# One transformer-style layer on one core: conditioning products on VectorE, complex products by three real ones, another order of steps

## The chip, the cores and the metric

The kernel runs on one core of a Trainium2 chip. The metric is the device time of one execution in microseconds (us). The engines are TensorE (matmul; PE in the rows, its weight loads PEld), VectorE (DVE), ScalarE (ACT), GpSimd (POOL) and SyncE (SP), which here only issues loads. Each engine runs its own queue in order and waits on semaphores for the others.

## The reference

One layer over 256 latent tokens and 256 context tokens of width 1024, all in fp32:

```
mod  = silu(c) @ w_mod + b_mod           # six vectors: shift1, scale1, gate1, shift2, scale2, gate2
h    = layer_norm(x) * (1 + scale1) + shift1          # the context likewise, with c_ctx
u, q, k, v, gates = split(h @ w_in)      # widths 512, 1024, 256, 256, 2048
y    = two-way S5 scan of u (32 groups, 64 complex states), started from the context's last states
ssm  = (gelu(y) @ w_glu_a) * sigmoid(gelu(y) @ w_glu_b)
att  = attention(q, k, v; latent and context keys) @ w_attn_o
x    = post_norm(alpha * x + gate1 * ((s1 * ssm + s2 * att) @ w_out))        # s1, s2 = sigmoid(gates)
m    = layer_norm(x) * (1 + scale2) + shift2
x    = post_norm(alpha * x + gate2 * moe(m))   # 32 experts, a token goes to 2 of them
```

The context needs shift1 and scale1 only; shift2, scale2, gate1 and gate2 are products of `c` alone ("c-only").

## The kernel before, in words

The program has two phases. The first, everything up to the routing, is written as some 45 generators ("streams"), such as `loads`, `mod2`, `w2_flow`, `scan`, `dense`, `outputs`, `prefetch4`. A stream yields `ask(engine, tiles, ...)` ahead of each step, and class `Flow` resumes one stream at a time. Which one is a fixed list of stream numbers, `ORDER`; where each tile lies in the area of SBUF is a second list, `PLACE` (NS places of 4 KB a partition). So the order of each engine's queue, and of the loads in SP's, is decided when the program is built. All engine calls of this phase pass through one helper, so their rows carry one line, L273.

The parts that matter here:

- `mod_loads` and `mod_cols` (L437 to L606) make the mod vectors. For each of 12 groups TensorE multiplies 16 blocks of w_mod (256 columns) by a 32-column tile that holds silu of c and of c_ctx (`scp`), in fp32, two passes each; ScalarE copies the result (`mr`), TensorE turns it by four transposes, VectorE sums the parts (`msum`) and adds the bias. `mod1` does the four groups of shift1 and scale1; `mod2` the eight c-only groups.
- `s5_powers`, `w1_flow`, `w2_flow` (L705 to L906) build the scan's matrices on VectorE: 16 blocks, each a complex product of powers (`pin`, `pout`) with b or c, as six operations of 128x512.
- The dense products (`dense`, L1238) run as three matmuls on fp32r halves. `split` makes the halves: ScalarE copies the high one, VectorE subtracts for the low one, TensorE then takes both.
- `u_turn` (L673) sends u through DRAM (`uscr`) with loads on POOL's queue. `outputs` (L993) turns each block of the scan's output on TensorE, writes it to DRAM (`yscr`) and reads it back as `yT`, where ScalarE applies GELU.
- `prefetch8`, `prefetch2`, `prefetch4` and `refill` load 18 pieces of expert weights, 1 MB each, into places as they come free.

The second phase (from L1861) is a loop over 16 pairs of experts. For each pair: the gate product (`into(p, 0)`, tiles `gu`), the combination of the last pair's result, the up product (`into(p, 1)`), the dispatch of the next pair's tokens, the down product (`down_of`, tiles `y`); `reload` issues the next weights as places come free. In the last pair `ln2_row` (L1852) spreads the final norm's gain and bias over the partitions by one-row matmuls, and `overflow` (L1756) holds a branch that handles experts with too many tokens. Then the final norm runs on VectorE and four stores end the program.

Of the kernel before, what the change touches and what calls it, by code (L numbers as in the profile page):

```python
# [86 lines left out]
class Flow:  # L87
# [247 lines left out]
def build(ctx, tc, I, out):  # L335
# [549 lines left out]
    def w1_flow():  # L885
        for b in range(8):
# [1125 lines left out]
```

## Time and profile before

| | us |
|---|---|
| time, median of 3 runs (lowest, highest) | 813.92 (812.88, 816.1) |
| the profiled execution, its own time | 813.46 |
| its span in the trace | 811.6 |
| busy: TensorE, VectorE, ScalarE, POOL | 762.1, 370.8, 294.2, 30.9 |

Mean granted TensorE clock 0.984 of full speed; HBM read 265.79 MB. Times in rows are us from the span's start unless marked ns. A busy share is an average over stages that are limited by different things, so the stages have to be read apart. An engine's idle time is shown with the instruction that ended it ("<-"); matmuls overlap, so their busy time can be a little over the time from start to start.

### The profile page before, as it was taken

How to read it: one execution, taken by the hardware profiler on the slowest of the kernel's cores; microseconds unless marked ns; L12 is line 12 of the kernel's file. 1: busy time of each engine (PE TensorE's matmuls, PEld its weight loads, DVE VectorE, ACT ScalarE, POOL GpSimd, SP SyncE). 2: the span in 40 equal slices, each digit the busy share in tenths (PEclk: the TensorE clock that was granted, in tenths of full speed). 3: DMA queues.
4: the chain of work that ended last, by engine and by line, in shares of the span. 5: the costliest groups of instructions: out<-in, count | busy, mean ns of one | idle time of the engine just before them, and what ended most of it. 6: DMA issues, size and time to landing. Idle time of an engine off the chain costs nothing. (4 is left out here: it accounts for less than half of the span.)

```text
span 811.6 us, 11217 instructions
## 1 busy us (share of the span) xinstructions
PE 762.1 (94%) x4371; PEld 435.6 (54%) x4371; DVE 370.8 (46%) x858; ACT 294.2 (36%) x573; POOL 30.9 (4%) x48
## 2 busy tenths in 40 slices
PE   3899989889999999899999999999999999999985
PEld 1678677657657787744444444444344434443422
DVE  6999978888634768723112211221222112211205
ACT  4552586856988543432212210221022102211210
POOL 0003312000000000200000000000000000000000
PEclk9999999999999999799999999999999999999998
DMA  9987364594478886959999999999999999999991
GB/s 352 350 303 262 87 231 137 212 333 136 152 181 333 329 286 240 367 187 391 423 422 422 421 420 421 420 419 422 422 420 420 422 421 420 422 420 420 422 372 53
DMA packets 52126, 269.70 MB, mean 332 GB/s; under 512 B 10082, under 2 KB 15586, under 8 KB 23268
## 3 DMA queue, kind: packets, MB, share of 16 engines
q1 hardware_dynamic: 46260, 265.28, 82.3%
q0 software_dynamic: 1152, 2.59, 1.1%
q10 hardware_dynamic: 4656, 1.05, 0.7%
q8 instruction: 37, 0.61, 0.3%
q14 instruction: 21, 0.17, 0.1%
HBM read 265.79 MB, written 3.11 MB: 331 GB/s over the span
## 5 line engine op out<-in xcount | busy, mean ns | idle before, releaser
L273 PE MATMUL gu<-b,b 128*64 128x512 f32 x1024 | 231.0, 597 | 3.4 <-DMA b<-in_w_exp_up_dram 2.6
L273 PE MATMUL acc<-b,b 128*128 128x512 f32 (+1 forms) x792 | 202.4, 390 | 4.4 <-DVE q L273 2.0
L273 PEld LDWEIGHTS acc<-b,b 128*128 128x128 f32 x792 | 136.5, 190 | 36.2 <-issue 9.2
L273 PEld LDWEIGHTS gu<-b,b 128*64 128x64 f32 x1024 | 73.3, 137 | 148.3 <-issue 138.6
L273 PE MATMUL y<-b,hT 128*64 128x512 f32 x512 | 113.4, 595 | 0.2 <-issue 0.2
L273 DVE TENSOR_TENSOR hh<-hh,gu 128x512 f32<-128x512 f32 (+1 forms) x17 | 11.0, 655 | 213.8 <-PE gu L273 193.0
L273 ACT ACTIVATE b<-y,modT 128x128 f32<-128x128 f32 x120 | 45.2, 456 | 138.5 <-PE y L273 138.5
L273 DVE TENSOR_TENSOR b<-b,b 128x1024 fp32r<-128x1024 f32 (+1 forms) x61 | 72.0, 1187 | 30.8 <-ACT b L273 29.7
L273 ACT ACTIVATE b<-b 128x1024 fp32r<-128x1024 f32 (+3 forms) x70 | 71.3, 1028 | 26.5 <-PE acc L273 24.2
L273 PEld LDWEIGHTS y<-b,hT 128*64 128x64 f32 x512 | 35.8, 137 | 66.5 <-issue 66.5
L273 PEld LDWEIGHTS y<-d,b 128*128 128x128 f32 x480 | 55.9, 192 | 12.2 <-issue 11.4
L273 PE MATMUL y<-d,b 128*128 128x128 f32 x480 | 60.0, 278 | 0.0
L273 ACT ACTIVATE yh<-b 128x512 fp32r<-128x512 f32 x31 | 19.5, 629 | 97.5 <-DVE b L273 97.5
L273 DVE SCALAR_TENSOR_TENSOR b<-y,wsl,b 128x512 f32<-128x512 f32 x32 | 24.0, 751 | 66.2 <-PE y L273 66.2
L273 ACT ACTIVATE hh<-gu 128x512 f32<-128x512 f32 x16 | 9.6, 597 | 117.0 <-PE gu L273 117.0
L273 ACT ACTIVATE b<-tr 128x512 f32<-128x512 f32 (+2 forms) x60 | 33.9, 583 | 49.4 <-PE tr L273 48.7
L273 PE MATMUL ss<-b,b 128*32 128x128 f32 (+2 forms) x344 | 36.9, 305 | 4.6 <-ACT b L273 2.9
L273 PE MATMUL acc<-b 128*128 128x512 f32 (+1 forms) x104 | 36.9, 368 | 0.0
L273 PEld LDWEIGHTS ss<-b,b 128*32 128x32 f32 (+1 forms) x344 | 25.9, 147 | 14.8 <-issue 8.7
L273 DVE TENSOR_TENSOR yl<-b,yh 128x512 fp32r<-128x512 f32 x31 | 21.5, 692 | 23.3 <-ACT yh L273 23.3
L273 PE MATMUL ss<-b,scp 128*32 128x256 f32 x384 | 26.8, 414 | 5.0 <-DMA b<-in_w_mod_dram 5.0
L273 PE MATMUL acc<-yh,cw 128*128 128x512 f32 x62 | 26.1, 421 | 0.0
(209 smaller groups left out, 675.7 us busy)
## 6 DMA issues: line engine op xcount, KB each, us to landing
b<-in_w_exp_gate_dram SPq DMA_DIRECT2D x64, 1024.0 KB, 19.8
b<-in_w_exp_up_dram SPq DMA_DIRECT2D x64, 1024.0 KB, 19.8
b<-in_w_exp_down_dram SPq DMA_DIRECT2D x63, 1024.0 KB, 19.8
b<-in_w_mod_dram SPq DMA_DIRECT2D x32, 512.0 KB, 7.0
b<-in_w_in_dram SPq DMA_DIRECT2D x14, 1024.0 KB, 7.7
b<-in_w_mod_dram SPq DMA_DIRECT2D x8, 1024.0 KB, 8.6
b<-in_w_attn_o_dram SPq DMA_DIRECT2D x4, 1024.0 KB, 5.3
b<-in_w_out_dram SPq DMA_DIRECT2D x4, 1024.0 KB, 5.0
```

What stands on the lines that cost most here:

```text
L273: return f(*args, **kw)
```

## The change

- **c-only products on VectorE.** `mod2` no longer uses TensorE. The c-only part of w_mod is stored transposed (`w_modT`, 32 tiles of 128x1024, 512 KB each); SP loads c once, spread over all partitions (`crow`), ScalarE applies SiLU, and 32 VectorE operations multiply a tile by it and sum along the row. The tiles are loaded from half of the scan on, into places of kind p4. `gate1`, `router_w` and `diag2` wait for the vectors that they use.
- **Complex products by three real ones.** Each of the 16 blocks takes one operation of 512 and two of 1024 elements a partition; sums and differences of the powers are made ahead (two operations on POOL, 12 copies on ScalarE, two on VectorE).
- **U by one load** of 1 MB on SP's queue in place of four on POOL's.
- **Gated output on TensorE.** The scan's output is gathered in `ya`, and eight transposes feed GELU straight from PSUM; `yscr` goes, and w_glu's rows are stored in the order that this gives.
- **Order and space.** New `ORDER` and `PLACE`, 46 places, still 18 prefetched pieces; the attention's output product may start once its first part is there.
- **The end.** The final norm's gain and bias come as two broadcast loads of 512 KB behind the last weights, not by `ln2_row`; the overflow test stands ahead of the last up product; in the final norm ScalarE sums one half of the tokens.

```diff
@@ mod_loads, mod2
-        for o in ((3, 4), (2, 5)):
-            for jp in range(4):
-                yield ask("Z", None, lambda: m_l[0] == 4, lambda: U, g4=4)
-                wm.append([[wload(w_mod, z * D + 256 * jp, 256, k0, 4, "g4") for k0 in (0, 4)] for z in o])
+        for z in (1, 2, 0, 3):
+            for j in range(KT):
+                yield ask("Z", None, lambda: m_l[0] == 4, lambda: g_n[0] >= 15, p4=1)
+                r = new("p4", [P, D], name="wr")
+                SY.dma_start(r, I["w_modT"][z * KT + j])
+                wm2.append(r)
...
-        for half in (1, 2):
-            for jp in range(4):
-                yield ask("T", None, lambda: mod_n[0] >= 4)
-                yield from mod_cols(half, jp)
+        yield ask("Y", None, lambda: m_l[0] == 4, lambda: g_n[0] >= 14, p4=1)
+        cb = new("p4", [P, D], name="cb")
+        bcast(cb, I["crow"], D)
+        yield ask("S", [cb], table=AF.Silu)
+        S.activation(cb, cb, AF.Silu)
+        for half, w in ((1, 0), (1, 1), (2, 0), (2, 1)):
+            sm = small.tile([P, KT], FT, name=f"msum{half}{w}", bufs=1)
+            for j in range(KT):
+                yield ask("V", lambda: [wm2[0], cb], lambda: wm2)
+                r = wm2.pop(0)
+                V.tensor_tensor_reduce(out=r, in0=r, in1=cb, scale=1.0, scalar=0.0, op0=OP.mult, op1=OP.add, accum_out=sm[:, j:j + 1])
+                free(r)
+            stt(modT[:, half, w, :, 0], sm, float(w if half < 2 else 0), bmodT[:, half, w], OP.add, OP.add)
+            md.add((half, w))
@@ w2_flow (w1_flow likewise)
-                for r in range(2):
-                    tt(t1, pr[0], cr[r], OP.mult)
-                    tt(w2[:, r], pr[1], cr[1 - r], OP.mult)
-                    if r == 0:
-                        tt(w2[:, 0], t1, w2[:, 0], OP.subtract)
-                    else:
-                        stt(w2[:, 1], t1, -1.0, w2[:, 1], OP.mult, OP.subtract)
+                tt(t1, pone[0][:, 0, i, :, :, None].to_broadcast(ps4), sums[0][:, 0, i, :, None, :].to_broadcast(ps4), OP.mult)
+                tt(w2.rearrange("p r g j c -> p (r g) j c"), pout[0][:, i].rearrange("p r g j -> p (r g) j")[:, :, :, None].to_broadcast(sh),
+                   s5c[0][:, i].rearrange("p r g c -> p (r g) c")[:, :, None, :].to_broadcast(sh), OP.mult)
+                tt(wf, wf, t1.rearrange("p g j c -> p (g j c)")[:, None, :].to_broadcast([P, 2, 512]), OP.add)
@@ u_turn
-        for i in range(4):
-            PL.dma_start(U[0][:, 8 * i:8 * i + 8], ...)
+        SY.dma_start(U[0], bass.AP(tensor=uscr.tensor, offset=uscr.offset, ap=[[64, P], [16 * 512, G], [1, 64]]))
@@ outputs
-                T.transpose(ps, yk, ident)
-                S.activation(ysb[:, 4 * b:4 * b + 4], ps.rearrange("p (g k) -> p g k", g=4), AF.Copy)
-            S.dma_start(bass.AP(tensor=yscr.tensor, ...), ysb)
-        S.dma_start(y_, yscr.rearrange("(i p) t -> p i t", p=P))
-        S.activation(y_, y_, AF.Gelu_apprx_tanh)
+                S.activation(ya[:, :, 4 * f + b], ps.rearrange("p (j c) -> p j c", j=8), AF.Copy)
+        for z in range(2):
+            for j in range(4):
+                T.transpose(ps[:, j], ya[:, 4 * z + j].rearrange("p g c -> p (g c)"), ident)
+            S.activation(yv[:, 4 * z:4 * z + 4], ps.rearrange("p j (i k) -> p j i k", i=4), AF.Gelu_apprx_tanh)
@@ the last pair and the end
+        else:
+            overflow(gu_p.tile([P, F], FT, name="gu"))
         into(p, 1, range(UB))
-        if not more:
-            for i in range(3):
-                lnp = ln2_row(i, gu_p if i == 2 else y_p)
         into(p, 1, range(UB, KT))
...
-            overflow(lnp)
+            ln2 = unit(D)[1]
+            for z in range(2):
+                bcast(ln2[:, z], I["ln2_b" if z else "ln2_g"], D)
...
+        S.activation(sq[n][:, 0:512], acc[1][n], AF.Copy, accum_out=s4[:, 0, n:n + 1])
+        S.activation(sq[n][:, 512:], acc[1][n], AF.Square, bias=mv[1][:, 1:2], accum_out=s4[:, 1, n:n + 1])
```

How the queues change, at three places. First TensorE, among the gate projections, where the scan's kernels (`kall`) are turned. Before (`scp` is the tile of silu of c, `mr` the copied result, `acc` the projections):

```order
L273 MATMUL acc<-b_117,b_247 128x512
L273 MATMUL ss<-b_107,bm 32x128 x8
L273 MATMUL ss<-b_107,scp 32x256 x4
L273 MATMUL ss<-b_113,scp 32x256 x4
L273 MATMUL ss<-b_123,scp 32x256 x4
L273 MATMUL ss<-b_337,scp 32x256 x4
L273 MATMUL tr<-kall,cst_78 128x64
L273 MATMUL acc<-b_117,b_336 128x512
L273 MATMUL acc<-b_458,b_336 128x512
L273 MATMUL acc<-b_117,b_247 128x512
L273 MATMUL tr<-cst,mr 128x128 x4
```

With the change, at the same turn of `kall`:

```order
L284 MATMUL acc<-b_290,b_513 128x512
L284 MATMUL acc<-b_348,b_513 128x512
L284 MATMUL tr<-kall,cst_78 128x64
L284 MATMUL acc<-b_210 128x512
L284 MATMUL acc<-b_211,b_210 128x512
L284 MATMUL acc<-b_210,b_211 128x512
```

The `scp` matmuls and `mr` transposes are gone from between the projections; the four groups of `mod1` are the only ones left, all in the first 113 entries of the queue.

Second VectorE with the change, in the attention stage behind the scan (`ISA` is the multiply-and-sum and, in the short rows, the reading of its sum into `msum`; `b_1561` is silu of c; the `TENSOR_TENSOR` rows of 128x1024 are low halves of splits):

```order
L284 TENSOR_TENSOR b_290<-b_1682,b_2272 128x1024
L284 ISA b_122,msum_2165<-b_122,b_1561 128x1024
L284 ISA msum_2165 128x1
L284 ISA b_425,msum_2165<-b_425,b_1561 128x1024
L284 RECIPROCAL sm<-sm 128x2
L284 TENSOR_TENSOR b_210<-b_425,b_2082 128x1024
L284 ISA b_105,msum_2165<-b_105,b_1561 128x1024
L284 SCALAR_TENSOR_TENSOR modT<-msum_2165,bmodT 128x8
L284 TENSOR_TENSOR b_2359<-b_1399,b_2359 128x1024
```

(Each multiply-and-sum is followed by such a short row; one stands here.) Before, no such rows stood between the low halves; 30 of the 32 stand behind the scan now.

Third SP, between the first expert loads. Before:

```order
L273 DMA b_115<-in_w_exp_gate_dram 128x2048
L273 DMA b_337<-in_w_glu_a_dram 128x2048
L273 DMA b_2709<-in_w_glu_b_dram 128x2048
L273 DMA count<-in_count_dram 128x256
L273 DMA rt<-in_wr_dram 128x288
L273 DMA rt<-in_br_dram 128x36
L273 DMA b_107<-in_w_exp_gate_dram 128x2048
L273 DMA b_1081<-in_w_exp_gate_dram 128x2048
L273 DMA b_575<-in_w_exp_up_dram 128x2048
```

With the change:

```order
L284 DMA b_2377<-in_w_modT_dram 128x1024
L284 DMA b_915<-in_w_exp_gate_dram 128x2048
L284 DMA b_441<-in_w_glu_b_dram 128x2048
L284 DMA b_207<-in_w_modT_dram 128x1024
L284 DMA b_1399<-in_w_glu_a_dram 128x2048
L284 DMA b_2448<-in_w_exp_gate_dram 128x2048
L284 DMA b_1637<-in_w_attn_o_dram 128x2048
L284 DMA b_425<-in_w_exp_up_dram 128x2048
L284 DMA b_151<-in_w_modT_dram 128x1024
```

The loads of `w_modT` stand between the expert loads and those of the glu weights; before, all of w_mod had been loaded ahead of them. Ten of the 18 expert loads come behind the last of them.

## Rows read from the trace of the kernel before

**Rows 1.** Windows by stage: us, busy of each engine (instructions), PEclk, DMA share, GB/s.
```profile
core 0: us, PE busy (x) PEld busy (x) DVE busy (x) ACT busy (x) POOL busy (x), PEclk, DMA share, GB/s
0.00:58.00 58.00, 39.68 (x373) 30.68 (x374) 49.29 (x147) 31.81 (x56) 2.52 (x8) 0.97 0.91 347
58.00:212.00 154.00, 144.20 (x1010) 108.42 (x1010) 133.51 (x359) 99.17 (x205) 22.29 (x32) 0.99 0.57 192
212.00:347.00 135.00, 127.67 (x706) 94.44 (x704) 83.40 (x153) 82.06 (x133) 4.99 (x6) 0.96 0.78 282
347.00:366.00 19.00, 17.96 (x94) 8.49 (x96) 4.00 (x16) 5.11 (x13) 0.00 (x0) 1.00 0.50 177
366.00:766.00 400.00, 398.54 (x2070) 181.21 (x2068) 86.57 (x161) 71.79 (x163) 0.00 (x0) 1.00 1.01 419
766.00:798.40 32.40, 30.17 (x119) 10.74 (x115) 4.39 (x8) 3.65 (x6) 0.00 (x0) 0.95 0.74 299
798.40:811.60 13.20, 3.90 (x11) 1.59 (x10) 9.68 (x17) 0.60 (x1) 1.10 (x2) 0.80 0.21 79
```
**Rows 2.** Windows again, the first microseconds of the first gate product.
```profile
350.00:354.00 4.00, 3.93 (x19) 1.40 (x20) 0.00 (x0) 1.06 (x4) 0.00 (x0) 1.00 0.01 4
```
**Rows 3.** Groups by line, TensorE, 58 to 213 us: xcount | busy, mean ns | idle before.
```profile
L273 PE MATMUL ss<-b,scp 128*32 128x256 f32 x256 | 16.1, 383 | 2.3 <-DMA b<-in_w_mod_dram 2.3
L273 PE MATMUL tr<-cst,mr 128*128 128x128 f32 x32 | 4.8, 274 | 0.0
```
**Rows 4.** Groups by line and form, VectorE and ScalarE (the second row: 212 to 347 us).
```profile
L273 DVE TENSOR_TENSOR wt<-pout,b 128x512 f32<-128x512 f32 x16 | 11.0, 687 | 0.2
L273 DVE TENSOR_TENSOR b<-b,b 128x1024 fp32r<-128x1024 f32 x30 | 36.5, 1224 | 27.9 <-ACT b L273 27.1 <-PE acc L273 0.5
L273 DVE SCALAR_TENSOR_TENSOR b<-b,dnv,b 128x1024 f32<-128x1024 f32 x2 | 2.6, 1276 | 0.0
L273 ACT ACTIVATION_READ_ACCUMULATOR pe<-acc,mx,rq 128x1 f32 x16 | 3.1, 196 | 0.0
L273 ACT ACTIVATE b<-ss 64x256 f32<-64x256 f32 x32 | 19.9, 622 | 6.0 <-PE ss L273 5.6
```
**Rows 5.** Timeline of VectorE, two places: start us, us, what, [idle before].
```profile
77.25 0.68 DVE L273 SCALAR_TENSOR_TENSOR b<-wt,b 128x512 f32<-128x512 f32 x1
77.85 0.68 DVE L273 TENSOR_TENSOR w<-wt,w 128x512 f32<-128x512 f32 x1
...
83.61 1.23 DVE L273 TENSOR_TENSOR b<-b,b 128x1024 fp32r<-128x1024 f32 x1
84.76 0.69 DVE L273 SCALAR_TENSOR_TENSOR b<-wt,b 128x512 f32<-128x512 f32 x1
```
**Rows 6.** Waits of VectorE, 212 to 347 us: us in total, times, longest.
```profile
DVE b L273 <- ACT b L273: 28.4, 23, 3.7
DVE sm L273 <- ACT pe L273: 9.2, 3, 5.0
```
**Rows 7.** DMA issues: xcount, KB each, median us from issue to landing.
```profile
b<-uscr POOLq DMA_DIRECT2D x4, 256.0 KB, 4.4
...
b<-yscr ACTq DMA_DIRECT2D x1, 512.0 KB, 4.0
```
**Rows 8.** Windows again, where the scan's output goes through DRAM.
```profile
240.00:260.00 20.00, 20.00 (x88) 14.59 (x87) 9.61 (x12) 17.27 (x27) 0.00 (x0) 1.00 0.74 269
```
**Rows 9.** Timeline of TensorE and VectorE at the end.
```profile
781.45 1.93 PE L273 MATMUL gu<-b,b 128*64 128x512 f32 x6 [1.31 <-DMA b<-in_w_exp_up_dram]
783.31 1.98 PE L273 MATMUL y<-b,count 1*128 1x512 f32 x4
786.38 3.29 PE L273 MATMUL gu<-b,b 128*64 128x512 f32 x8
...
804.54 0.69 DVE L273 BATCH_NORM_STATS2 fst<-acc 128x6 f32<-128x512 f32 x1
```
**Rows 10.** Windows again, in the last up product.
```profile
786.00:788.00 2.00, 2.00 (x5) 0.53 (x6) 0.00 (x0) 0.60 (x1) 0.00 (x0) 0.50 0.92 357
```
**Rows 11.** Timeline of TensorE, the first gate product of the expert phase.
```profile
350.07 2.37 PE L273 MATMUL gu<-b,b 128*64 128x512 f32 x10 [0.60 <-ACT b L273]
```

More of the change, by code (lines that the diff above doesn't have):

```diff
@@ L792, in s5_powers @@
             yield ask("V")
-            tt(b_[:, r], dd[:, 0], dd[:, 1], OP.add if r else OP.subtract)
-            yield ask("V")
+            d0, d1 = (dd[:, z].rearrange("p (b g) c -> p b g c", g=4) for z in range(2))
+            if r:
+                stt(b_[:, :, 1], d0, -1.0, d1, OP.mult, OP.subtract)
+            else:
+                tt(b_[:, :, 0], d0, d1, OP.subtract)
+            yield ask("V", **({"p4": 1} if r else {}))
         free(dd, s5b[0])
+        sums.append(new("p4", [P, 2, 8, 4, C], name="sums"))
+        tt(sums[0][:, 1], b_[:, :, 0], b_[:, :, 1], OP.add)
         bb.append(b_)
@@ L1377, in prefetch4 @@
     def prefetch4():
-        for i in range(5):
+        for i in range(7):
             yield ask("Z", None, None, room("p4", 2), p4=2)
@@ L1394, in gate1 @@
     def gate1():
[L1395 removed]
+        yield ask("V", None, lambda: g1 and (2, 0) in md and count)
         yield from grow(0, g1[0])
@@ new lines, in build @@
+    sq = os_[2:]
+    st = small.tile([P, 2, 6], FT, name="fst")
+    mv = [small.tile([P, 2], FT, name=f"fmv{a}", bufs=1) for a in range(2)]
+    rs = [small.tile([P, 1], FT, name=f"fr{a}", bufs=1) for a in range(2)]
+    s4 = small.tile([P, 2, 2], FT, name="fs4", bufs=1)
+    for n in range(2):
+        V.bn_stats(st[:, n], acc[0][n])
+        S.activation(sq[n][:, 0:512], acc[1][n], AF.Copy, accum_out=s4[:, 0, n:n + 1])
+    V.bn_aggr(mv[0], st)
+    rsqrt(rs[0], mv[0][:, 1:2], EPS)
+    tt(mv[1][:, 0:1], s4[:, 0, 0:1], s4[:, 0, 1:2], OP.add)
@@ new lines, in build, with half @@
+    V.tensor_scalar(mv[1][:, 1:2], mv[1][:, 0:1], -1.0 / D, None, op0=OP.mult)
+    for n in range(2):
+        S.activation(sq[n][:, 512:], acc[1][n], AF.Square, bias=mv[1][:, 1:2], accum_out=s4[:, 1, n:n + 1])
+    def half(a, z):
+        cs_ = slice(512 * z, 512 * z + 512)
+        o = os_[a][:, cs_]
+        if a == 0:
+            stt(o, acc[a][z], mv[0][:, 0:1], ln2[:, 0, cs_], OP.subtract, OP.mult)
+        else:
+            stt(o, acc[a][z], mv[1][:, 1:2], ln2[:, 0, cs_], OP.add, OP.mult)
+        yield
+        stt(o, o, rs[a], ln2[:, 1, cs_], OP.mult, OP.add)
+        SY.dma_start(out[a * P:(a + 1) * P, cs_], o)
+        yield
@@ L1954, in layout @@
+    h = [half(a, z) for a in range(2) for z in range(2)]
+    for g_ in (h[0], h[0], h[1], h[1]):
+        next(g_)
+    tt(rs[1], s4[:, 1, 0:1], s4[:, 1, 1:2], OP.add)
+    V.tensor_scalar(rs[1], rs[1], 1.0 / D, EPS, op0=OP.mult, op1=OP.add)
+    PL.tensor_tensor(out=rs[1], in0=rs[1], in1=mhalf[:, 0:1], op=OP.pow)
+    for g_ in (h[2], h[2], h[3], h[3]):
+        next(g_)
 def layout(inputs):
```

205 lines of the change are left out of this document (93 added, 112 removed), and 11 rows, old and new, of the table PLACE.

## The prediction

> **What bounds the kernel now.** I read the table of windows by stage first [rows 1], because a share over the whole span mixes stages with different limits. From 366 to 766 us, fifteen of the sixteen expert pairs, TensorE is busy 398.54 of 400 us and the DMA share is 1.01: both are full, and the change touches neither there. Just before, from 350 to 354 us, the DMA share is 0.01 [rows 2]: every place for weights is taken and the queue stands still. So the expert phase runs on a reserve of loaded weights, and if it starts s us earlier with the same reserve, the end comes s us earlier. Ahead of it two stretches count. From 58 to 212 us TensorE is busy 144.20 of 154 us and VectorE 133.51, with a DMA share of 0.57. From 212 to 347 us TensorE is busy 127.67 of 135, VectorE only 83.40, and DMA 0.78. TensorE is the bound of both, so TensorE work taken out there should show; VectorE is the runner-up early and has 51.6 us idle late. The profiled execution took 813.46 us (span 811.6), 0.46 under the median of the runs shown, 813.92. A measurement of this kernel can tell about 0.5% from no change: 4.1 us, so 809.9 and 818.0 are the borders of "same".
>
> **c-only products, what goes.** Eight groups of 32 matmuls and four transposes leave TensorE between 58 and 213 us: 16.1 + 4.8 = 20.9 us busy, and in front of them 2.3 us of waiting for w_mod [rows 3]. Their matmuls overlap a little at the seams, so I count busy time alone and not the wait: **-21 us**. Bounds: -23.2 with the wait, and about -11 if VectorE takes over as the early bound, since it falls by only that much (next part).
>
> **Complex products.** Sixteen blocks of six 512-element operations become sixteen of one with 512 and two with 1024. A 512 one takes 687 ns, and the next starts 0.60 us after it (77.25 to 77.85); a 1024 one takes 1224 ns, and the next starts 1.15 after it (83.61 to 84.76) [rows 4, 5]. So 96 x 0.60 = 57.6 us become 16 x (0.60 + 2 x 1.15) = 46.4: -11 us of VectorE work, beside TensorE, not on its path. This is what lets TensorE's -21 show: without it VectorE, at 133.51 of the old 154, would be fuller than the shortened 133. The twelve ScalarE copies that lay out the powers cost 12 x 0.62 = 7.4 us by the nearest row [rows 4], on an engine busy 99.17 of 154; they delay the first block by some 5 us, which I price at 0 because projection matmuls stand ready for TensorE then; if they do not, +5.
>
> **c-only products, what comes.** Thirty-two VectorE multiply-and-sum operations over 128x1024, each with a small instruction that reads the sum, 30 of them behind the scan. No row shows this form. Low end: 1.15 us as the plain product; plus 0.20 for the read, by ScalarE's accumulator read [rows 4]: 1.35. High end: twice the product and a read, 2.5, if the sum takes a pass of its own. I take 1.35, since the nearest rows, a product and a two-operation form on the same shape, differ by only 1224 against 1276 ns [rows 4]. That is 30 x 1.35 = 40.5 us for a stretch with 51.6 idle. But of those 51.6, VectorE spends 28.4 waiting for ScalarE's high halves of a split and 9.2 for softmax sums, in pieces of at most 3.7 and 5.0 us [rows 6]: 37.6 of waiting, 14.0 of free time. So 26.5 us, some 20 operations, must fit into waits, and each, once started, makes the low half of a split late for the matmuls behind it. I take a quarter of an operation, 0.3 us, for each: **+5 us**. Bounds: 0 if all fit, +26.5 if none do.
>
> [...]
>
> **The loads that move.** 32 loads of 512 KB, 16.8 MB, leave the stretch with share 0.57 and enter the one with 0.78, on SP's queue between the expert loads, where one waiting for its place holds up those behind. Room: at the 419 GB/s of the expert phase, 135 us carry 56.6 MB; 282 GB/s were used, 38.1 MB; left 18.5, and 347 to 366 us, at 177 GB/s, leaves 4.6 more [rows 1]. 16.8 fits into 23.1: **0**, with little over; what does not fit costs 1 us for 0.42 MB.
>
> **U by one load; gated output on TensorE.** U moves from POOL's queue to SP's, where it waits for U's scratch writes with projection loads behind it; a piece lands 4.4 us after issue [rows 7], early, while other projection work is there: 0, at most +4. The trip of the output through DRAM (a read of 512 KB lands in 4.0 us [rows 7]) lies at 240 to 260 us, where TensorE is busy 20.00 of 20 [rows 8]; it hid nothing and waits for nothing. Transposes are eight before and eight after. 0 both ways.
>
> **The end.** [...] The overflow test moves ahead of the last up product, where TensorE already waits 1.31 us for weights [rows 9]: 0. The two 512 KB broadcasts that replace the rows come behind the last weights and are needed after 12 us: 0. Of the closing VectorE chain two statistics of 0.69 us [rows 9] go to ScalarE, which adds hand-overs of its own: **-0.6**, bounds 0 and -1.4.
>
> **Sum.** 813.46 - 21 + 5 - 4 - 0.6 = 792.9, so **793 us**; against the median it would be 793.3. Its own range from the bounds: 787 to 803.
>
> **Rivals.** First, **VectorE sets the early stretch**: it was nearly as full as TensorE, and its split loop feeds TensorE in order. Then -11 stands for -21: 803 us. Against it: only 2.3 of TensorE's early waits were on one named releaser, w_mod.
>
> Second, on the slower side, **VectorE becomes the bound of the late stretch**. Place: the splits between 212 and 347 us; price: 30 operations of p us each. Without any late cost the time is 788; it comes back to 813.5 when VectorE's excess is 25.6 us. If no wait can be filled, only 14.0 us are free and the point is p = (14.0 + 25.6) / 30 = 1.32; if all can, it is (51.6 + 25.6) / 30 = 2.57. With p = 2.5, 75 us, the excess is 23.4 to 61.0, the time 811 to 849, the middle 830. [...] With p = 1.35 and no wait filled it is 788 + 26.5 = 814, no change. For it: the splits wait in a loop of three engines. Against it: the sums depend on nothing but their load, so the list can put them into any wait.
>
> Third, **expert weights come late**: if half of the 16.8 MB finds its place only after the scan's tail and pushes as much of the reserve behind it, 8.4 - 4.6 = 3.8 MB are missing, 9 us: 802 us, with waits for expert weights in the first pairs.
>
> Fourth, **more goes than the rows name**: early, TensorE idles 9.8 us, and a new order with -11 on VectorE may close it, with the late cost nearer 0: 776 to 788, say 781.
>
> That the c-only products stay on TensorE is excluded: only the first half's four groups are in its queue.
>
> **How the numbers follow.** Forecast 0.53; early stretch bound by VectorE 0.10; late weights 0.12; more than named 0.12; VectorE late at 2.5 us 0.07; at 1.35 with unfilled waits 0.06. Faster: the first four, 0.87, less 0.02 for overshoot past 809.9: 0.85. Slower: 0.07, of which 0.01 falls inside the border, and 0.02 of the 814 case beyond it: 0.08. Same: 0.07. The range goes from 778 (most of the fourth rival) to 812, leaving out the slower side, 0.13, and the low end of the fourth, 0.04.
>
> **What would show it.** Right: the early stretch some 20 us shorter at TensorE 0.93 or more; the new operations near 1.3 us with reads of 0.2; VectorE near 120 busy of the late 135, TensorE's new waits on its low halves adding a few us; the first gate product of pair 0 near 334 instead of 350.07 [rows 11]; DMA no longer idle just after it; the last down product 4 us earlier against that start. Wrong: a mean near 2.3 us, TensorE waiting tens of us on VectorE after the scan, or waits for expert weights in the first pairs.

## The result, and the profile after

The changed kernel takes **803.22 us** (median of 3 runs, 801.58 to 805.22) against 813.92: 10.7 us less by the medians. The ratio over the runs, by which the experiments below are compared too, is 0.9881, 95% interval 0.9849 to 0.9914; at 813 us that is 9.7 us. Either way it is faster and inside the range, but only about half of the 20.9 us forecast. Its profiled execution has a span of 801.4 us.

Windows of the changed kernel by stage, columns as in [rows 1]. The first three are those of [rows 1] moved 8 us earlier, though the scan does not end at the same place in them. The last three rows divide the time up to the first expert product where the same work stands in both kernels: at the start of the scan's last step (195.0 us; 211.5 before) and at the first sigmoid of the gated unit (GLU):

```profile
58.00:204.00 146.00, 131.63 (x784) 98.35 (x783) 134.85 (x333) 108.17 (x215) 20.09 (x28) 0.98 0.44 145
204.00:339.00 135.00, 126.19 (x655) 93.37 (x645) 110.55 (x203) 77.60 (x119) 4.98 (x6) 0.94 0.96 359
358.00:758.00 400.00, 397.46 (x2064) 182.11 (x2062) 86.02 (x161) 71.80 (x163) 0.00 (x0) 1.00 1.01 418
...
342.00:346.00 4.00, 4.00 (x20) 1.48 (x21) 0.00 (x0) 0.96 (x3) 0.00 (x0) 1.00 0.00 0
...
58.00:195.00 137.00, 123.68 (x709) 92.81 (x707) 127.07 (x319) 99.39 (x204) 20.09 (x28) 0.98 0.42 137
195.00:254.60 59.60, 52.95 (x361) 35.11 (x362) 42.29 (x71) 43.59 (x66) 0.00 (x0) 0.94 0.92 316
254.60:341.96 87.36, 83.21 (x376) 65.65 (x375) 78.53 (x159) 43.52 (x67) 4.98 (x6) 0.94 0.94 368
```

The expert phase is unchanged (TensorE 397.46 of 400, DMA 1.01), and the DMA queue again stands still behind the first gate product (342 to 346, share 0.00, as in [rows 2]). So the gain is made ahead of it. The late window, 204 to 339, has the loads (share 0.96 where it was 0.78) and the sums (VectorE 110.55 where it was 83.40), as meant, and its clock is lower: 0.94 for 0.96. The kernel before, cut at the same work (its middle part, 48.80 us, stands further down):

```profile
58.00:211.50 153.50, 143.70 (x1008) 107.96 (x1007) 133.05 (x356) 98.67 (x204) 22.29 (x32) 0.99 0.57 193
...
260.30:350.07 89.77, 84.79 (x379) 66.71 (x377) 66.77 (x133) 41.97 (x65) 4.99 (x6) 0.94 0.79 302
```

The early stretch is thus 16.5 us shorter (137.0 for 153.5), with TensorE busy 0.90 of it. From the scan's last step to the first expert product it is 8.4 us longer (147.0 for 138.6): 10.8 longer up to the sigmoid and 2.4 shorter behind it.

Timeline of the changed kernel's TensorE, the first gate product and the end:

```profile
341.96 3.65 PE L284 MATMUL gu<-b,b 128*64 128x512 f32 x16 [0.60 <-ACT b L284]
...
765.29 3.65 PE L284 MATMUL gu<-b,b 128*64 128x512 f32 x16
772.31 7.09 PE L284 MATMUL gu<-b,b 128*64 128x512 f32 x32 [3.37 <-PEq L1799]
780.08 0.41 PE L284 MATMUL y<-cst,hh 128*128 128x128 f32 x2 [0.68 <-DVE hh L284]
...
781.05 7.09 PE L284 MATMUL y<-b,hT 128*64 128x512 f32 x32 [0.23 <-issue]
```

The first gate product comes at 341.96 for 350.07 [rows 11], 8.1 us earlier (the forecast: 334). From there to the end of the span it was 811.6 - 350.07 = 461.5 us and is 801.4 - 341.96 = 459.4: 2.1 less. The broadcast matmuls of [rows 9] are gone, but TensorE now stands 3.37 us ahead of the last up product, released by its own sequencer (PEq) at line 1799, the branch of the overflow test.

Groups by line of the changed kernel, VectorE, 0 to 341.96 us, columns as in [rows 3]:

```profile
L284 DVE TENSOR_TENSOR b<-b,b 128x1024 fp32r<-128x1024 f32 x57 | 69.4, 1221 | 15.8 <-ACT b L284 15.6
L284 DVE CUSTOM_DVE_ANT_0 b<-b,b 128x1024 f32<-128x1024 f32 x30 | 36.4, 1219 | 0.4 <-DMA b<-in_w_modT_dram 0.3
L284 DVE DVE_READ_ACCUMULATOR2_ANT msum<- 128x1 f32 x32 | 2.6, 83 | 0.0
```

The multiply-and-sum (the second row) takes as long as a plain product, 1219 beside 1221 ns, and the read of its sum 83 ns: 1.30 together, where 1.35 was taken.

### The profile page after: what moved, and what is told of

Same layout as the page of the kernel before. It is cut to its first block, busy times and chain, and to the rows that moved or that the text cites. A ratio compares the mean times of both kernels' runs of the same rounds, so it can differ in the third digit from the quotient of the medians.

```text
span 801.4 us, 10609 instructions
## 1 busy us (share of the span) xinstructions
PE 744.4 (93%) x4075; PEld 428.4 (53%) x4075; DVE 390.8 (49%) x852; ACT 305.9 (38%) x581; POOL 30.8 (4%) x46
## 5 line engine op out<-in xcount | busy, mean ns | idle before, releaser
L284 PE MATMUL gu<-b,b 128*64 128x512 f32 x1024 | 228.7, 594 | 6.5 <-PEq L1799 3.4
L284 PE MATMUL acc<-b,b 128*128 128x512 f32 (+1 forms) x752 | 193.6, 390 | 6.0 <-ACT b L284 3.8
L284 PEld LDWEIGHTS gu<-b,b 128*64 128x64 f32 x1024 | 75.0, 137 | 147.7 <-issue 138.8
L284 PEld LDWEIGHTS acc<-b,b 128*128 128x128 f32 x752 | 132.7, 193 | 38.6 <-issue 7.7
L284 ACT ACTIVATE b<-b 128x1024 fp32r<-128x1024 f32 (+2 forms) x70 | 71.4, 1029 | 39.0 <-PE acc L284 16.9
L284 DVE TENSOR_TENSOR b<-b,b 128x1024 fp32r<-128x1024 f32 (+1 forms) x65 | 74.6, 1156 | 15.9 <-ACT b L284 15.6
L284 PEld LDWEIGHTS y<-d,b 128*128 128x128 f32 x480 | 55.9, 192 | 12.2 <-issue 11.4
L284 PE MATMUL acc<-b 128*128 128x512 f32 (+1 forms) x144 | 57.2, 421 | 3.8 <-ACT b L284 2.1
L284 DVE CUSTOM_DVE_ANT_0 b<-b,b 128x1024 f32<-128x1024 f32 x30 | 36.4, 1219 | 0.4 <-DMA b<-in_w_modT_dram 0.3
L284 PEld LDWEIGHTS acc<-b 128*128 128x128 f32 x144 | 27.5, 195 | 11.9 <-ACT b L284 2.9
## 6 DMA issues: line engine op xcount, KB each, us to landing
b<-in_w_mod_dram SPq DMA_DIRECT2D x8, 1024.0 KB, 10.1
b<-in_w_out_dram SPq DMA_DIRECT2D x4, 1024.0 KB, 10.1
```

Of the source, the lines that this page charges most:

```text
L284: return f(*args, **kw)
```

## The experiments

Two theories stood against each other: the c-only products' 21 us were worth less than their busy time (because VectorE, or another engine, was close behind: the first rival), or they were worth it and the sums gave it back. Ratios are to the kernel before in the same batch, with their 95% interval; "first product" is the first gate product of pair 0, in the profiled execution.

**c-only products off TensorE, alone.** In the kernel before, all of the c-only work on TensorE (the matmuls, copies and transposes of `half` 1 and 2) is left out:

```diff
@@ before, mod_cols
+        if half:
+            free(*r[0], *r[1])
+            yield ask("T")
+            j = slice(2 * jp, 2 * jp + 2)
+            for w in range(2):
+                stt(modT[:, half, w, j], bmodT[:, half, w, j, None].to_broadcast([P, 2, 2]), ...)
+            mod_n[0] += 1
+            return
```

> The kernel before, in its own order and with all its loads, without the eight c-only groups on TensorE (matmuls, copies and transposes left out; those four vectors are made of the bias alone). If TensorE's queue is what the early stretch waits for, as forecast, 20.9 us of work and 2.3 of waiting go: -18 to -22 us against before, 792 to 796. If VectorE and ScalarE set that stretch and TensorE's c-only work only filled its waits: -8 or less, 806 or more, with TensorE's waits on them up by as much. [...]

Measured: first product 340.62, 9.5 us earlier than before's. The whole takes 1108 us: without these products the routing differs, the overflow test is true and its body runs. The end can therefore not be compared, and the next pairs of kernels also multiply the overflow count by 0.

**The changed kernel without its sums**, with and without their loads (a_no_sum_load shortens each load to 64 of 1024 columns):

```diff
@@ after, mod2
-                V.tensor_tensor_reduce(out=r, in0=r, in1=cb, ..., accum_out=sm[:, j:j + 1])
...
-            stt(modT[:, half, w, :, 0], sm, ...)
+            stt(modT[:, half, w, :, 0], bmodT[:, half, w], ...)
```

> The changed kernel without its 32 multiply-and-sum operations on VectorE (the loads and the order stay; the four vectors are made of the bias alone). VectorE loses about 40 us behind the scan. By the forecast they cost 5 us on the path: 797 to 800. If VectorE's place in the split loop is where the missing 10 us went: 788 to 794. If they cost nothing and the loss lies elsewhere: 801 to 804.

> As the kernel without the sums, and with each of the 32 c-only loads cut to one sixteenth (64 of 1024 columns): 16 MB less to move behind the scan. If those loads hold up others in SP's queue or on the DMA engines, another 3 us or more below the kernel without the sums; if there was room for them, as the forecast has it, the same within 1.5 us.

Measured: first product 330.67 without the sums, 333.26 without loads as well (totals 1106 and 1105, by the same branch). In these traces the sums cost about 11 us, and their loads nothing.

**The same two with the overflow count at 0**, so that whole times compare:

```diff
-        V.tensor_copy(total, cum[0:1, NE - 1:NE])
+        V.tensor_scalar(total, cum[0:1, NE - 1:NE], 0.0, None, op0=OP.mult)
```

> The kernel before without the c-only groups on TensorE, as b_no_mod, with the number of tokens beyond an expert's places multiplied by zero, so that the branch of the overflow is not taken and the whole time can be compared. From the first expert product of b_no_mod, 340.62 us against 350.07: about -9.5 against before, 802 to 805. If the 20.9 us counted in full and that trace was a bad one: 792 to 796.

> The changed kernel without the 32 sums, as a_no_sum, with the overflow's count multiplied by zero. From the first expert product of a_no_sum, 330.67 us against 341.96: -11 against the changed kernel, 791 to 793. If the sums cost the 5 us of the forecast: 797 to 799.

Measured: b_no_mod0 803.61, 0.9892 (0.9871 to 0.9913); a_no_sum0 793.98, 0.9768 (0.9745 to 0.9791). At 813 us these give the account: products off TensorE -8.8 (-10.5 to -7.0); all else but the sums -10.1; the sums +9.2 (0.9881 - 0.9768), the last two with some 3 us either way by the intervals. Window of the kernel before from 0 to its first product:

```profile
0.00:350.07 350.07, 313.58 (x2102) 235.40 (x2102) 268.69 (x668) 213.76 (x395) 29.80 (x46) 0.98 0.70 251
```

The same of b_no_mod0:

```profile
0.00:339.91 339.91, 299.22 (x1814) 227.17 (x1814) 266.54 (x660) 209.39 (x387) 29.75 (x46) 0.97 0.72 258
```

TensorE's busy time falls by 14.4 us. Weighted with the granted clock, read in windows of 2 us, its work at full clock falls from 305.6 to 289.9 us, by 15.7. Its idle time (window less busy) rises from 36.5 to 40.7. That is how 20.9 us of busy records became 10: some 5 were not there, as the rows of groups overlap (for 58 to 213 us of the kernel before they add up to 169.1 us, in a window with 145.20 busy), 4.2 came back as waiting and some 1.4 as lower clock. The scan's last step comes 11.0 us earlier than before (200.5 for 211.5), so of the changed kernel's 16.5 another 5.5 are made by the rest of the change.

**Is VectorE the successor?** Five kernels take VectorE work out of the early stretch. a_no_third is the changed kernel without the third operation of its 16 complex blocks (-18 us of VectorE); b_no_mod_dve is b_no_mod0 without the 32 operations that combine products (-19 us); in b_no_mod_scan (made from b_no_mod0), b_scan (from the kernel before) and a_scan (from the changed one) each scan step has two operations for four. Each leaves that part of the result out; all but a_no_third have the overflow count at 0.

```diff
@@ a_no_third (w2_flow, w1_flow)
-                tt(wf, wf, t1.rearrange(...)..., OP.add)
@@ b_no_mod_dve (w2_flow, w1_flow)
-                    if r == 0:
-                        tt(w2[:, 0], t1, w2[:, 0], OP.subtract)
-                    else:
-                        stt(w2[:, 1], t1, -1.0, w2[:, 1], OP.mult, OP.subtract)
...
-                tt(w1[r], t1, w1[r], OP.add if r else OP.subtract)
@@ the scan
-            tt(y2, g_[:, k, ::-1], apn[:, 0], OP.mult)
-            tt(y1, y1, sb[0][:, k], OP.add)
-            tt(g_[:, k + 1], y1, y2, OP.add)
+            tt(g_[:, k + 1], y1, sb[0][:, k], OP.add)
```

> The changed kernel without the last of the three operations in each of the 16 blocks of the complex products (the addition of 1024 elements left out, so the scan's matrices are not complete): 16 x 1.15 = 18.4 us less on VectorE ahead of the scan. If VectorE sets the early stretch: -8 to -18, 785 to 795. If TensorE sets it: within 2 us of the changed kernel, 801 to 804.

> The kernel before without the c-only groups on TensorE (as b_no_mod0) and also without the combining operation in each half of the 16 blocks of the complex products (32 operations of 512 elements, about 19 us of VectorE ahead of the scan; the scan's matrices are not complete). If VectorE was what kept the 20.9 us of TensorE work from showing in full: -5 to -12 against b_no_mod0, 792 to 799. If it was something else, waits in the chain of small steps: within 2 us of b_no_mod0, 802 to 805.

> The kernel before without the c-only groups on TensorE (as b_no_mod0) and with the scan's 31 serial steps cut from four VectorE operations to two (imaginary cross term left out; the overflow's count multiplied by zero): about 15 us less on VectorE between 165 and 201 us. If the c-only work only filled TensorE's waits while VectorE ran the scan and the softmax's maxima stood behind it, the cut shows now: 6 us or more below b_no_mod0, 798 or less. If not: within 2 us, 802 to 805.

> The kernel before, with its c-only groups on TensorE, and only the scan's steps cut from four operations to two (overflow's count multiplied by zero). If TensorE with the c-only work is the bound of that stretch: within 3 us of before, 810 to 814. If VectorE already set it there: as far below before as b_no_mod_scan is below b_no_mod0.

> The changed kernel with the scan's steps cut from four operations to two (overflow's count multiplied by zero). If the scan on VectorE is what the changed kernel waits for: 6 us or more below it, 797 or less; if the loss lies only in the sums behind the scan: within 3 us, 800 to 805.

Measured: a_no_third 803.03, 0.9881 (0.9837 to 0.9926): nothing. b_no_mod_dve 804.84, 0.9906 (0.9871 to 0.9941): nothing against 0.9892. b_no_mod_scan 801.31, 0.9876 (0.9851 to 0.9902); b_scan 813.19, 1.0022 (0.9996 to 1.0048); a_scan 800.14, 0.9889 (0.9828 to 0.9951): nothing that can be told from noise. (a_scan is the least certain: its interval is wide, and in its trace the first product comes at 336.90, 5.1 us earlier than the change's.) So the complex products' time on VectorE is not what holds the early stretch; for the scan a few us stay possible. The window of b_no_mod_dve to its first product:

```profile
0.00:341.20 341.20, 303.68 (x1813) 231.13 (x1814) 247.18 (x628) 209.26 (x387) 29.26 (x46) 0.94 0.71 257
```

With 19.4 us less of VectorE, TensorE idles less (37.5 us for 40.7) and runs more at half clock (0.94 for 0.97 on the mean; 15 windows of 2 us at 0.50 or 0.51 for 7), in an execution of 808.08 us, 3.2 above the median. Its three longest waits between 58 us and the scan's end are for other links than the products (a softmax step of ScalarE, and two small VectorE results that come at the end of chains):

```profile
121.64 0.41 PE L273 MATMUL tr<-cst,kk 128*128 128x128 f32 x2 [1.59 <-DVE kk L273]
...
148.66 0.47 PE L273 MATMUL acc<-b,b 128*128 128x512 f32 x1 [1.97 <-DVE q L273]
...
170.28 2.12 PE L273 MATMUL acc<-b,b 128*128 128x512 f32 x3 [3.52 <-ACT pe L273]
```

The opposite, 19 us of VectorE work added to the changed kernel behind its 16 blocks:

```diff
@@ a_add_early (w2_flow; w1_flow likewise)
+                V.tensor_reduce(out=t1[:, 0, 0, :1], in_=w2.rearrange(...), axis=AX.X, op=OP.add)
```

> The changed kernel with a useless row sum of 1024 elements behind each of the 16 blocks of the complex products (same output): about 19 us more on VectorE ahead of the scan. The kernel with 18 us less was not faster. If VectorE has room there, 802 to 806; if it stands just under the bound, so that less gains nothing but more shows: +8 to +19, 811 to 822.

Measured: 820.78, 1.0099 (1.0068 to 1.0130), first product 361.36. Against 0.9881 that is +17.7 us for 19: no reserve upwards. In the changed kernel's order VectorE stands just under the bound.

**The size of the sums' cost.** Half as long (sums over 512 of the 1024 elements, overflow count at 0), and with a second sum over each tile (+38 us of VectorE):

```diff
@@ a_half_sum0
+                V.tensor_tensor_reduce(out=r[:, :512], in0=r[:, :512], in1=cb[:, :512], ...)
@@ a_double_sum
+                V.tensor_reduce(out=sm[:, j:j + 1], in_=r, axis=AX.X, op=OP.add)
                 V.tensor_tensor_reduce(...)
```

> The changed kernel with each of the 32 sums over 512 of the 1024 columns (the vectors are partial sums; the overflow's count is multiplied by zero): about 18 us less on VectorE behind the scan, the same number of steps. If the sums cost by VectorE's time, half of the 9 us that the kernel without them gained: 798 to 800. If they cost by standing in the queues between the others' steps: within 1.5 us of the changed kernel, 802 to 804.

> The changed kernel with a second, useless row sum of the same tile in front of each of the 32 (same output): about 38 us more on VectorE behind the scan. If VectorE is the bound there now: 20 to 38 us slower, 823 or more. If the cost goes on as it did for the first 39 us, one quarter shows: about +9, 812. If it is covered: 803 to 805.

Measured: a_half_sum0 800.16, 0.9839 (0.9793 to 0.9884): -3.4, though the interval reaches the changed kernel's. a_double_sum 831.51, 1.0230 (1.0188 to 1.0272): +28.4 us for 38. So the late stretch covers about three quarters of the sums' 39 us (their reads not counted), and of anything beyond them only a quarter. The place is the attention stage. Windows from the scan's last step to the first GLU sigmoid, a_no_sum0 (after's, 59.60 us, stands in its table above):

```profile
195.00:246.40 51.40, 49.17 (x361) 33.19 (x362) 21.35 (x34) 43.44 (x67) 0.00 (x0) 1.00 0.98 346
```

The same 361 matmuls take 8.2 us longer with the sums, which is nearly all of the 9.2: TensorE idles 4.4 us more and is busy 3.8 more, as the clock falls from 1.00 to 0.94. With half sums the stretch took 56.1 us (193.5 to 249.6), midway. The same stretch of the kernel before:

```profile
211.50:260.30 48.80, 45.40 (x349) 30.05 (x348) 19.58 (x34) 41.33 (x73) 0.00 (x0) 1.00 0.70 226
```

The changed kernel ends its scan 16.5 us earlier (195.0 for 211.5) and has 5.7 left of it at the sigmoid (254.6 for 260.3): this is where the gain was spent. One link, from the changed kernel's timeline (VectorE, ScalarE, TensorE):

```profile
239.57 1.22 DVE L284 CUSTOM_DVE_ANT_0 b<-b,b 128x1024 f32<-128x1024 f32 x1
...
240.72 0.08 DVE L284 DVE_READ_ACCUMULATOR2_ANT msum<- 128x1 f32 x1
240.84 1.06 ACT L284 ACTIVATE b<-b 128x1024 fp32r<-128x1024 f32 x1 [2.44 <-DVE msum L284]
...
243.13 1.28 ACT L284 ACT_TABLE_LOAD   x1
...
244.43 1.09 ACT L284 ACTIVATE b<-acc 128x512 f32<-128x512 f32 x2
...
245.08 5.07 PE L284 MATMUL acc<-b,b 128*128 128x512 f32 x14 [3.01 <-ACT b L284]
```

ScalarE waits 2.44 us with the high half of a split, because, by the releaser that the profile names, its place comes free only with the sum that read it. A softmax step, a table load and the copies of the attention's output stand behind it in ScalarE's queue, and TensorE waits 3.01 us for these. That is most of the 4.4 us; its next wait, 2.15 us at 217.14, ends by the profile with a DMA of `w_modT` (without the sums TensorE waits 1.2 us there for `kscr`). The forecast had looked for late low halves on VectorE; the longest wait came through ScalarE and a place.

**The sums shared with GpSimd**: every second one multiplied there and summed by ScalarE.

```diff
@@ a_pool_half, mod2
+                if j % 2:
+                    PL.tensor_tensor(out=r, in0=r, in1=cb, op=OP.mult)
+                    S.activation(r, r, AF.Copy, accum_out=sm[:, j:j + 1])
```

> The changed kernel with every second of the 32 multiply-and-sum operations done in two: POOL multiplies (128x288 takes it 0.80 us, so some 2.8 us for 1024), ScalarE adds up along the row (about 1.25 us). VectorE loses some 19 us behind the scan, as in a_half_sum0, with the same output. If VectorE's time is the price of the sums: -3 to -5, about 799. If ScalarE, which gets 20 us, stands in the same loop: within 2 us of the changed kernel or above it, 802 to 808.

Measured: 817.54, 1.0053 (1.0021 to 1.0086): all of the gain lost. Groups by line, 0 to its first product at 355.41:

```profile
L284 POOL TENSOR_TENSOR b<-b,b 128x1024 f32<-128x1024 f32 x15 | 37.3, 2487 | 117.3 <-DMA b<-in_w_modT_dram 103.2 <-ACT b L284 8.4 <-PE tr L284 5.6
L284 DVE TENSOR_TENSOR b<-b,b 128x1024 fp32r<-128x1024 f32 x57 | 78.8, 1386 | 26.0 <-ACT b L284 25.7
```

GpSimd needs 2487 ns for a product, and VectorE's low halves rise from 1221 to 1386 ns on the mean. ScalarE got the 16 row sums as well; the run does not part the three.

**The half clock**: short matmuls into scratch results fill TensorE's named waits, four of them in a_fill_all (14, 18, 13 and 5 matmuls), two in a_fill_mid (6 and 10):

```diff
@@ a_fill_mid, outputs and attention values
+                for _ in range(6 if (f, b) == (1, 0) else 0):
+                    T.matmul(ps, ident, ident, start=True, stop=True)
...
+            for _ in range(10 if o_n[0] == 2 else 0):
+                T.matmul(ps[:, 0], ident, ident, start=True, stop=True)
```

> The changed kernel with useless matmuls put in front of work that TensorE waits for at three places: 14 and 18 of 128x128 at 217 and 242 us (the first output block of the second half, the third attention value product), 13 of 128x36 and 5 of 128x128 in the router at 324 and 327 us. They add about 6 us of TensorE work. If a wait of some 2 us costs another 1.7 to 5 us because the clock granted behind it is half, the clock stays up at these places and the time falls by 3 to 8 us in spite of the added work: 795 to 800. If the clock has another cause, or the waits are the whole cost: the same, or up to 6 us slower, 803 to 809.

> The changed kernel with useless matmuls in two waits only, 6 of 128x128 at 217 us and 10 at 242 us, shorter than the waits (2.15 and 3.01 us; 28 rows took 3.29 us and 36 took 4.18 in a_fill_all). If the two stretches at half clock behind these waits are on the path: -2 to -4, 799 to 801. If not: within 1.5 us of the changed kernel, 802 to 805.

Measured: a_fill_all 809.35, 0.9955 (0.9935 to 0.9976), slower by 6 than the change; its first product comes at 342.71, 0.8 later than the change's, so most of the loss is behind it (two stalls at the end, below). a_fill_mid 802.30, 0.9876 (0.9843 to 0.9909): no change that can be told. Windows of the two places, the changed kernel and then a_fill_mid:

```profile
216.00:222.00 6.00, 4.86 (x35) 3.40 (x36) 3.60 (x9) 4.16 (x9) 0.00 (x0) 0.72 0.98 378
242.00:249.00 7.00, 3.99 (x11) 3.16 (x11) 6.97 (x10) 6.58 (x9) 0.00 (x0) 0.76 0.85 315
```

```profile
216.00:222.00 6.00, 6.00 (x75) 4.47 (x73) 4.65 (x11) 4.58 (x9) 0.00 (x0) 1.00 1.00 398
242.00:249.00 7.00, 6.22 (x25) 4.28 (x24) 6.46 (x12) 6.94 (x10) 0.00 (x0) 1.00 0.65 246
```

The clock rises to 1.00 and the end does not move by anything that can be told. In a_fill_mid's trace the stretch from the scan's last step (196.0) to the sigmoid (252.1) is 56.2 us for 59.6, so a gain of up to some 3 us at these two places, which the interval allows, is not excluded.

**The end**: the overflow test back behind the last up product, and the kernel before with the new end alone:

```diff
@@ a_late_if
-        else:
-            overflow(gu_p.tile([P, F], FT, name="gu"))
...
+            overflow(lnp)
```

b_new_end is the kernel before with the piece "the last pair and the end" of the change's diff and its closing statistics, and nothing else.

> The changed kernel with the overflow test behind the last up product, as it stood before, and nothing else undone. TensorE stood 3.37 us at this branch. If that is on the path: -3, about 800; if the last weights, still landing at 784 us, take its place: within 1.5 us of the changed kernel.

> The kernel before with only the new end: gain and bias of the last norm by two broadcast loads, the overflow test ahead of the last up product, ScalarE's sums in the final norm. The forecast has -4.6: 808 to 810. In the traces the part from the first expert product to the end was 461.5 us before and 459.4 with the change, since TensorE stood 3.4 us at the branch: then -2, 811 to 812.

Measured: a_late_if 805.76, 0.9910 (0.9882 to 0.9939), not to be told from 0.9881. b_new_end 811.44, 0.9994 (0.9965 to 1.0022): -0.5, between -2.8 and +1.8, where -4.6 was forecast. TensorE at the end, first a_late_if, then b_new_end:

```profile
779.98 0.41 PE L284 MATMUL y<-cst,hh 128*128 128x128 f32 x2 [3.31 <-PEq L1799]
...
780.96 8.78 PE L284 MATMUL y<-b,hT 128*64 128x512 f32 x32 [0.34 <-issue]
```

```profile
775.46 8.71 PE L273 MATMUL gu<-b,b 128*64 128x512 f32 x32 [3.34 <-PEq L1761]
```

The branch stops TensorE for 3.3 us at either place, and in these two the product behind it takes 8.7 to 8.8 us for 7.09, with a granted clock of 0.75 in 780 to 782 us and 0.50 in 782 to 784 of a_late_if; the changed kernel's own, at 1.00, takes 7.09. By its trace b_new_end gained 2.3 us from the first expert product to the end (459.2 for 461.5), which the interval allows as well. In a_fill_all TensorE stands 3.32 us at the branch and, a few matmuls later, another 2.64, released by nothing named ("issue").

No kernel without something left out was faster than the change beyond its interval.

## Why the prediction was half right

- **What bounds the kernel: right.** The expert phase kept its form and its reserve of weights, and the end followed its start: 8.1 us earlier, plus 2.1 at the end.
- **c-only products, -21: the first step that failed.** Alone they are worth -8.8. Two parts. Rows of groups overlap, so that their busy times added up count too much: at full clock TensorE's work fell by 15.7. Of these some 5.5 came back as waiting (idle +4.2) and lower clock. The step took TensorE, busy 144.20 of 154, for a bound whose work comes off one for one; the early stretch is a chain through all engines, and TensorE was only its fullest.
- **The first rival** (VectorE sets the early stretch, 803) gave the time, but its mechanism fell: -18 and -19 us of VectorE gained nothing, with either order. That its number came out is luck. The case against it had looked at w_mod alone: of TensorE's 9.8 us of early idle time 3.4 were waits for VectorE and 4.1 for ScalarE. What holds the stretch with TensorE's work gone is not settled. The complex products alone are not it, and a shorter scan showed nothing clear of noise; the waits move from one link to another, and in b_no_mod_dve half clock took back what the shorter waits gave.
- **Complex products, new order, gated output and U: priced at 0 beyond letting the -21 show, the end at -4.6; together they measured -10.1.** The end has -0.5 of it, so these parts, ahead of the experts, made some 9 to 10 us that the sum did not have. Which of them did is open. a_add_early speaks for VectorE's -11: put back in the new order, 19 us cost 17.7, and at that slope 11 would be 10. b_no_mod_dve speaks against it: in the old order 19 us less gained nothing. So the -11 can have paid only together with the new order, and no run has either alone.
- **The sums, +5: the second step that failed, in size.** The duration was right (1.30 for 1.35), the cost was 9.2. (Some 20 operations of 0.3 us are 6, not 5; that is a small part of it.) The quarter of an operation for each that does not fit was too little: a sum holds not only VectorE but the place of its tile, for which ScalarE waits, as the one link above shows. How the 9.2 divides between places, VectorE's time and half clock was not measured. The second rival's mechanism, VectorE's sums making the late stretch wait, was thus at work, with 9.2 us where it had 23.4 to 61.0.
- **Loads, 0: right.** DMA share 0.96, no wait for expert weights in the first pairs, and nothing gained, with the sums left out, by loads of a sixteenth of the size. The third rival fell. The sign named for it, DMA no longer idle behind the first gate product, did not come: the share there is 0.00, the reserve was complete.
- **The end, -4 and -0.6: the third step that failed.** No run shows the -4, which stands for the matmuls of [rows 9] that spread gain and bias and for the clock of 0.50 behind them [rows 10]: the new end alone gained 0.5 by its ratio and 2.3 by its trace. Three of the four broadcasts, two rows each, went from there (the fourth stood at 801.18), and the branch's 3.3 took their place, ahead of the up product where 1.31 us of waiting for weights had been seen to cover it. A branch, which the profile doesn't count as busy, was taken at no price. Its new place is not what made the stall: put back, it takes 3.31.

By these ratios the miss is +12.2 (products), +4.2 (sums), +4.1 (end) against -9.6 (the order's gain, which no term had): 10.9 in all. The largest two nearly cancel, which is luck too, and each carries the few us of its intervals.

## What to carry to other kernels

Busy time on the fullest engine does not come off one for one: here 20.9 us of records were worth 8.8, in a stretch where VectorE was busy 133.51 of 154 us too. Measure a version with the work simply left out before the replacement is written. Work put "into the waits" of another engine can cost by the places that it holds, not by its duration alone (here ScalarE stood 2.44 us for one place): look who waits for the tile that it reads. When a part is left out, look whether the data still takes the same branch.

## What was not expected of the hardware

**The branch.** At the branch that jumps over the overflow body TensorE stands for 3.3 us (3.37 in the changed kernel, 3.31 in a_late_if, 3.34 in b_new_end, 3.32 in a_fill_all; 3.4 in a_no_third) while the DMA share is near 1 (1.01 and 1.03 in 768 to 772 us of the changed kernel, 1.00 in 776 to 780 of a_late_if). The kernel before has no such stall at its own branch, where TensorE waits 0.69 us for `hh`, a VectorE result, and the DMA queue has drained to a share of 0.21:

```profile
790.35 0.41 PE L273 MATMUL y<-cst,hh 128*128 128x128 f32 x2 [0.69 <-DVE hh L273]
...
790.00:792.00 2.00, 1.42 (x8) 0.81 (x10) 1.29 (x4) 0.00 (x0) 0.00 (x0) 1.00 0.21 76
```

In the stall of the changed kernel one packet of an instruction queue lands; a row of its DMA view, 768 to 770 us (queue, packets, MB, share):

```profile
q8 instruction: 1, 0.02, 3.3%
```

There are 33 such packets in the whole span, and the stalls of a_late_if, b_new_end and a_fill_all hold one each too, as does the second stall of a_fill_all. What makes TensorE stand there is not shown: no run here took the branch away, or changed only the DMA share or the packet at it. a_late_if rules out the branch's place.

**VectorE beside GpSimd.** In a_pool_half the timeline shows VectorE operations with two inputs of 128x1024 that run longer beside a product of GpSimd; POOL's and VectorE's rows:

```profile
236.40 2.87 POOL L284 TENSOR_TENSOR b<-b,b 128x1024 f32<-128x1024 f32 x1 [0.45 <-DMA b<-in_w_modT_dram]
...
248.09 2.36 POOL L284 TENSOR_TENSOR b<-b,b 128x1024 f32<-128x1024 f32 x1 [0.91 <-DMA b<-in_w_modT_dram]
```

```profile
236.95 3.40 DVE L284 CUSTOM_DVE_ANT_0 b<-b,b 128x1024 f32<-128x1024 f32 x1
...
248.26 3.28 DVE L284 TENSOR_TENSOR b<-b,b 128x1024 fp32r<-128x1024 f32 x1 [0.78 <-ACT b L284]
```

The sum that began at 236.95 took 3.40 us, 1.08 of it behind GpSimd's end at 239.27; the low half at 248.26 took 3.28, 1.09 of it behind 250.45. Both ended a little less behind the other engine than the 1.21 us that such an operation takes at 240.28, with GpSimd idle. Two more, a sum at 225.64 (2.31 us) and a low half at 235.56 (1.47 us), end 1.08 and 1.09 us behind GpSimd's end likewise. What holds VectorE in these four is not shown.

**The half clock without a wait.** In a_fill_all the router's stretch stayed at half clock (0.50) although TensorE was busy in it without a gap; a window of it:

```profile
330.00:334.00 4.00, 4.00 (x21) 4.00 (x20) 0.42 (x2) 2.72 (x8) 0.37 (x2) 0.50 1.01 420
```

The kernel before has half clock there too (338 to 341 us: busy 3.00 of 3, clock 0.50), but there TensorE had stood idle for 2.07 us, up to 335.17. So in these two windows a full row of busy time did not mean a full clock.
